# Making the split weight blocks of four tail pairs anew in the second half of a Strassen projection, instead of storing and reloading them

## The chip, the cores and the metric

One core of one Trainium2 chip runs the whole program. The metric is the time of one execution on the device in microseconds. The kernel before takes 2260.27 us, the median of 3 runs (2259.36 to 2262.28).

## What is computed

One layer of a residual decoder block on a sequence of 2048 rows of width 1024, in float32. Cut to what matters here:

```
h    = rms_norm(x) * (1 + scale) + shift
proj = h @ w_in                      # 1024 x 8192
x_rnn, z_rnn, q, k, v, z_attn, g_r, g_a = split(proj)
y_rnn  = (rg_lru(conv(x_rnn)) * silu(z_rnn)) @ w_out_rnn
y_attn = (dilated_attention(rope(q), rope(k), v) * silu(z_attn)) @ w_out_attn
merged = sigmoid(g_r) * y_rnn + sigmoid(g_a) * y_attn
out    = rms_norm(x + gate * (merged @ w_o))
```

The change touches only how the operands of `h @ w_in` and of `merged @ w_o` are prepared.

## The kernel before

**The products.** A float32 product is made of three passes over a high and a low part (`mm3`, L152). The high part is a rounded copy made on ACT (`hi_act`, L158), the low part a difference made on POOL (`lo_pool`, L164). All of `proj` but the values v is computed in 28 "pairs" of two 128-column blocks, by a Strassen scheme of 7 products a pair (`strassen`, L362; 12 matmuls of 128x512 each, L150, accumulated in PSUM tiles X, Z, W, V, Y). The sequence is done in two halves, f = 0 and f = 1, with the same 28 pairs, so that each half has 196 products, one after the other on PE. The first sums of a pair leave PSUM as tile u1 on ACT (L399) before the fifth product can use X again.

**The pairs.** Pairs 0 to 21 are the recurrent branch with the gates in between; the tail, pairs 22 to 27, makes q and k. In the tail (`TAIL_ROTATED`), pairs 23 and 25 hold the rotary columns, eight pieces of 32 columns (they go through `split` for all seven operands and are stored whole), and 22, 24, 26 and 27 are "plain", with blocks of one or two pieces of columns.

**The left operands.** In the first half they are made from the weight (`operand_events`, L265): four raw blocks of 256 KB loaded on SP (tiles R, L253), sums on DVE (s1, s2, L289, L290, and two in place, L298 and L303), seven splits (tiles S), each placed `LEAD` = 4 products ahead of its use. The splits are then stored to DRAM (sD, 512 KB each) from ACT's queue, each two splits after it was made (L281; the last two in a flush, L284). Operands 0, 4 and 5 of a pair that is not rotated are not stored (`PLAIN`), since they are split copies of raw blocks. In the second half `load_next` (L317) brings each operand into a ring of seven S tiles as soon as the product seven before it is done: from sD (L325), or the raw block (L253) with its split four products ahead (`split_next`).

**Between the halves** `second_values` (L863) computes v for the second half in eight runs (`value_runs`, L840). A run's two PSUM tiles are copied on ACT (ev, L767) and stored with four DMAs on SP (vN, L769) after the first quarter of the next run. The four first loads of the ring are in the plan at the first quarter of run 7, three more in the quarters behind.

**In the second half** two more jobs are spread between products: `output_weights` (L436) splits the output weights by way of the tiles s1 and s2 and stores them, 32 parts, one in 19/4 products; `gated_weight` (L1299) loads four groups of `w_o` (tiles wo, ws), multiplies them by the gate on DVE (L1315), forms Strassen sums, and stores them to oD (L1331, L1332) from ACT's queue. The groups begin 1, 10, 19 and 28 products into the tail.

**Queues.** SP and ACT issue their DMAs in program order. The compiled program gives each DMA of the two queues one of eight semaphores in turn (DMAHW0 to 7 in its waits), and a DMA first waits for the earlier DMA that holds the same one. A store on ACT's queue that waits so holds up all that ACT has behind it.

Of the kernel before, what the change touches and what calls it, by code (L numbers as in the profile page):

```python
# [10 lines left out]
F32 = mybir.dt.float32  # L11
# [4 lines left out]
ALU = mybir.AluOpType  # L16
# [4 lines left out]
P = 128  # L21
# [4 lines left out]
CH = 512  # L26
# [63 lines left out]
def decoder_block(ctx, tc, x, c, positions, g_norm, w_mod, b_mod, w_in, b_gate, conv_w, conv_b,  # L90
# [170 lines left out]
    LEAD = 4  # L261
    PLAIN = {0: (0, 0), 4: (0, 1), 5: (1, 1)}
    loaders, unsplit = {}, []

    def operand_events(x, pieces):  # L265

# [7 lines left out]

        def split(i, name):
            first[7 * x + i] = t = split_s(v[name])
            if i not in PLAIN or x not in loaders:
                kept.append((7 * x + i, t))
            if len(kept) > 2:
                k, t2 = kept.pop(0)  # L280
                nc.scalar.dma_start(sD[k], t2[:].bitcast(F32))  # L281
            while 7 * x + i == 28 * 7 - 1 and kept:
                k, t2 = kept.pop(0)
                nc.scalar.dma_start(sD[k], t2[:].bitcast(F32))  # L284
# [54 lines left out]


    def split_next(n):
        while unsplit and unsplit[0][0] <= n:
            _, t, r = unsplit.pop(0)
            hi_act(t[:, 0], r)
            lo_pool(t[:, 1], r, t[:, 0])
# [16 lines left out]
    def strassen(up, f, key, done):  # L362
# [8 lines left out]
        def take():  # L371
            if f:
                return (f, *loaded.pop(0))
            i = next(n_op)
            return f, i, first.pop(i)

        def prod(ps, b, first, last, op=None):
            f, i, s = op or take()
            bh, bl = B[b]
            for k in range(KH):  # L380
                mm3(ps[:], s[:, 0, k, :], s[:, 1, k, :], bh[:, k, :], bl[:, k, :],
                    first=first and k == 0, last=last and k == KH - 1, skip_group_check=True)
            n_prod[0] += 1
            if f:
                used.add(i)
                while n_loaded[0] - NS in used:
                    load_next()
                split_next(i + 4)
            run_late(n_prod[0])

        X = T(pj, [P, CH], F32, "X", bufs=2)
# [44 lines left out]
    def output_weights():  # L436

        parts = [(i, w, m, half) for i, w in enumerate((w_out_rnn, w_out_attn)) for m in range(KT) for half in range(2)]
        for x, (i, w, m, half) in enumerate(parts):
# [17 lines left out]
            for d, fn in ((1, load), (4, split), (6, store)):  # L457
                after_prod.setdefault(n_prod[0] + 19 * x // 4 + d, []).append(fn)

# [403 lines left out]
    def second_values():  # L863
# [5 lines left out]
        for i in range(4):  # L869
            for t in range(7):  # L870
                if t == 3:
                    plan[t, i].append(lambda i=i: load_piece(0, i))
                else:
                    n = t + 1 if t < 3 else t - 4
                    plan[t, i].append(lambda n=n, i=i: split_piece(n, i))
                    if n not in (2, 3) or t == 1:
                        plan[t, i].append(lambda n=n, i=i: load_piece(n + 1, i))
            plan[7, i].append(lambda i=i: [load_next() for _ in range(4 if i == 0 else 1)])
        plan[7, 2].append(lambda: split_next(0))
# [419 lines left out]
    def gated_weight(ep):  # L1299
# [5 lines left out]
        def group(k):  # L1305
# [11 lines left out]
            def sums(i):  # L1317
                if not i:
                    v["t"] = T(ep, [P, 3, CH], F32, "ws")
                    v["t3"] = T(wq, [P, KH, P], F32, "s1", bufs=1)  # L1320
# [72 lines left out]
    for f in range(2):  # L1393
# [15 lines left out]
        if f:  # L1409
            output_weights()  # L1410

        pump()
# [864 lines left out]
```

## Time and profile before

| | |
|---|---|
| median of 3 runs | 2260.27 us |
| profiled execution, its own time | 2258.11 us |
| its span | 2256.0 us |
| mean granted clock of TensorE | 0.992 |
| PE busy | 2201.3 us (98%) |
| DVE, ACT, POOL busy | 1456.7, 1294.0, 1215.1 us |
| DMA | 520.19 MB, mean 231 GB/s |
| stores of splits to sD, loads from it | 118 and 118, 512 KB each |

The first half's products end at 720 us or so, the values of the second half run until 829.6, and the second half's products from there until 1409. Attention, the output products and the last norm follow. A row of the timeline gives the start, the length, the engine with the line and the operation, the tiles written and read, and in brackets how long the engine stood idle before it and what ended that.

### The profile page before, as it was taken

The page shows a single profiled execution, that of the slowest core. Times are in us where ns is not written, and L with a number is a line of the kernel's source. Part 1 is how long each engine was busy: PE and PEld are TensorE (multiplying, and loading weights), DVE is VectorE, ACT ScalarE, POOL GpSimd, SP SyncE. Part 2 cuts the span into 40 slices and gives each one's busy share as a digit, 9 for nine tenths or more (in the row PEclk, how much of TensorE's full clock was granted, in tenths as well). Part 3 has the DMA queues.
Part 4 walks back from the last instruction along what each step waited for, and adds up shares of the span by engine and source line. Part 5 has one row for each costly group of instructions (what it writes and reads, how often), then busy time and mean ns, then how long its engine had stood idle before and what let it go on. Part 6 is the DMA issues. An engine that isn't in the chain of part 4 may idle for free.

```text
span 2256.0 us, 34354 instructions
## 1 busy us (share of the span) xinstructions
PE 2201.3 (98%) x11359; PEld 1845.6 (82%) x11359; DVE 1456.7 (65%) x2451; ACT 1294.0 (57%) x2560; POOL 1215.1 (54%) x902
## 2 busy tenths in 40 slices
PE   8999999999999999999999999999999999999898
PEld 5998888888877988888888887888989898977786
DVE  5578788778557664555645455467677878645776
ACT  3547767678533436666766611477677887632333
POOL 2277677676556344445445312356565656433786
PEclk9999999999999999999999999999999999999999
DMA  8354665565797647877787899989988888788553
GB/s 283 90 171 165 204 212 179 189 228 189 233 268 230 219 138 224 260 233 237 241 256 237 261 309 296 298 266 289 272 280 264 241 261 257 234 275 260 174 168 131
DMA packets 455433, 520.19 MB, mean 231 GB/s; under 512 B 90360, under 2 KB 333268, under 8 KB 454232
## 3 DMA queue, kind: packets, MB, share of 16 engines
q1 hardware_dynamic: 427492, 434.95, 63.6%
q10 hardware_dynamic: 27572, 83.00, 9.7%
q8 instruction: 90, 1.47, 0.3%
q14 instruction: 87, 0.71, 0.1%
q0 software_dynamic: 192, 0.05, 0.0%
HBM read 340.67 MB, written 177.21 MB: 230 GB/s over the span
## 4 chain that ended last, share of the span: by engine, by line
PE 48%; DMA 10%; DVE 3%; issue 3%; ACT 2%; POOL 2%; SPq 1%; ACTq 0%; POOLq 0%; DVEq 0%
PE X L150 9%; PE pj L150 9%; PE V L150 7%; PE W L150 4%; PE Z L150 4%; PE Y L150 4%; PE sc L150 4%; PE o L150 4%; DMA fg<-mrT 1%; DMA meT<-fg 1%; PE pg L150 1%; PE pT L1628 1%; DMA wo<-in_w_o_dram 1%; PE pT L1641 1%; DMA R<-in_w_in_dram 1%
## 5 line engine op out<-in xcount | busy, mean ns | idle before, releaser
L164 POOL TENSOR_TENSOR S<-R,S 128x512 fp32r<-128x512 f32 x278 | 408.2, 1473 | 402.8 <-ACT S L158 361.4
L150 PE MATMUL X<-T,S 128*128 128x512 f32 x1344 | 334.8, 398 | 10.4 <-ACT S L158 5.2
L150 PE MATMUL V<-T,S 128*128 128x512 f32 x1344 | 331.2, 395 | 0.0
L150 PEld LDWEIGHTS X<-T,S 128*128 128x128 f32 x1344 | 255.0, 190 | 72.1 <-ACT S L158 5.9
L150 PEld LDWEIGHTS V<-T,S 128*128 128x128 f32 x1344 | 252.3, 188 | 58.3 <-DVE ev L466 0.3
L150 PE MATMUL pj<-yh,S 128*128 128x512 f32 x848 | 287.8, 397 | 4.6 <-DMA S<-wD 3.9
L158 ACT ACTIVATE S<-R 128x512 fp32r<-128x512 f32 x278 | 170.7, 622 | 134.5 <-DMA R<-in_w_in_dram 111.8
L164 POOL TENSOR_TENSOR S<-s,S 128x512 fp32r<-128x512 f32 x108 | 165.9, 1537 | 128.7 <-ACT S L158 97.0
L150 PEld LDWEIGHTS pj<-yh,S 128*128 128x128 f32 x848 | 160.9, 190 | 37.9 <-DVE fg L1859 4.3
L1544 ACT ACTIVATE pp<-pp,st 128x256 f32<-128x256 f32 (+3 forms) x256 | 133.4, 523 | 75.2 <-DVE st L1543 74.8
L150 PE MATMUL pj<-yl,S 128*128 128x512 f32 x424 | 167.5, 395 | 2.1 <-DVE yl L167 1.2
L150 PE MATMUL Y<-T,S 128*128 128x512 f32 x672 | 165.5, 395 | 0.0
L150 PE MATMUL Z<-T,S 128*128 128x512 f32 x672 | 165.4, 395 | 0.0
L150 PE MATMUL W<-T,S 128*128 128x512 f32 x672 | 165.3, 395 | 0.0
L150 PEld LDWEIGHTS Z<-T,S 128*128 128x128 f32 x672 | 126.6, 188 | 29.7
L150 PEld LDWEIGHTS Y<-T,S 128*128 128x128 f32 x672 | 126.6, 188 | 29.3
L150 PEld LDWEIGHTS W<-T,S 128*128 128x128 f32 x672 | 126.4, 188 | 29.3
L158 ACT ACTIVATE S<-s 128x512 fp32r<-128x512 f32 x108 | 67.3, 623 | 109.7 <-DVE s L290 35.1
L167 DVE TENSOR_TENSOR ptl<-pT,pth 128x384 fp32r<-128x384 f32 (+1 forms) x160 | 97.8, 628 | 49.3 <-ACT pth L158 47.1
L960 DVE SCALAR_TENSOR_TENSOR xc<-xr,par,xc 128x512 f32<-128x512 f32 x96 | 96.6, 1006 | 50.2 <-ACT xc L954 48.0
L1543 DVE CUSTOM_DVE_ANT_0 pp<-sc,msk 128x256 f32<-128x256 f32 (+3 forms) x256 | 104.2, 449 | 37.2 <-PE sc L150 35.0
L164 POOL TENSOR_TENSOR kq<-kraw,kq 128x512 fp32r<-128x512 f32 (+1 forms) x64 | 101.3, 1593 | 41.7 <-ACT kq L158 41.7
(382 smaller groups left out, 4841.6 us busy)
## 6 DMA issues: line engine op xcount, KB each, us to landing
sD<-S ACTq DMA_DIRECT2D x118, 512.0 KB, 3.7
S<-sD SPq DMA_DIRECT2D x118, 512.0 KB, 5.1
S<-wD SPq DMA_DIRECT2D x100, 512.0 KB, 5.7
R<-in_w_in_dram SPq DMA_DIRECT2D x196, 256.0 KB, 4.1
wD<-s ACTq DMA_DIRECT2D x64, 256.0 KB, 4.9
T<-in_w_mod_dram SPq DMA_DIRECT2D x8, 1024.0 KB, 12.0
vN<-ev SPq DMA_DIRECT2D x64, 128.0 KB, 2.8
zaT<-ev SPq DMA_DIRECT2D x32, 256.0 KB, 2.8
```

The costliest lines, as they stand in the source:

```text
L150: nc.tensor.matmul(o, lhsT=l, rhs=r, start=st, stop=sp, **kw)
L158: nc.scalar.activation(o, i, AF.Copy)
L164: nc.gpsimd.tensor_tensor(o, i, h.bitcast(F32), ALU.subtract)
L167: nc.vector.tensor_tensor(o, i, h.bitcast(F32), ALU.subtract)
L960: nc.vector.scalar_tensor_tensor(xc, xr[:, i : i + CH], cw(i), xc, ALU.mult, ALU.add)
L1543: nc.vector.tensor_tensor_reduce(pdst, s_ps, mask, 1.0, 3e38, ALU.add, ALU.min, m_)
L1544: nc.scalar.activation(pdst, pdst, AF.Exp, bias=m_, scale=-1.0, accum_out=l_)
L1628: nc.tensor.transpose(pt[:, c0 + j * P : c0 + (j + 1) * P], pp[i][:, k * P : (k + 1) * P], ident)
L1641: nc.tensor.transpose(pt[:, c * P : (c + 1) * P], pp[:, half * P : (half + 1) * P], ident)
```

## The change

The operands of the plain tail pairs (`ANEW` = 22, 24, 26, 27) are not stored in the first half, and the second half makes them once more by `operand_events`, with raw loads, sums and splits 4 products ahead; the ring of loads pauses inside these pairs (`load_free`). `output_weights` goes at one part in 9/2 products instead of 19/4, so that the tiles s1 and s2 are free before pair 22. `second_values` puts three of the ring's first loads at the end of run 6's plan. `gated_weight` writes two of its sums in place in the wo tile, stores 2 times 512 KB a group, and its groups begin at 1, 11, 21 and 31.

```
+    ANEW = (22, 24, 26, 27)
...
         def split(i, name):
+            if f:
+                assert n_loaded[0] == 7 * x + i
+                n_loaded[0] += 1
             first[7 * x + i] = t = split_s(v[name])
-            if i not in PLAIN or x not in loaders:
+            if x not in ANEW and (i not in PLAIN or x not in loaders):
                 kept.append((7 * x + i, t))
-            if len(kept) > 2:
-                k, t2 = kept.pop(0)
-                nc.scalar.dma_start(sD[k], t2[:].bitcast(F32))
-            while 7 * x + i == 28 * 7 - 1 and kept:
+            while len(kept) > 2 or kept and x >= ANEW[0] and kept[0][0] < 7 * x + i - 1:
...
+    def load_free():
+        n = n_loaded
+        while n[0] - NS in used and not (n[0] < 28 * 7 and n[0] // 7 in ANEW):
+            load_next()
...
-                while n_loaded[0] - NS in used:
-                    load_next()
+                load_free()
                 split_next(i + 4)
             run_late(n_prod[0])
+            if f:
+                load_free()
+                split_next(i + 4)
...
-                after_prod.setdefault(n_prod[0] + 19 * x // 4 + d, []).append(fn)
+                after_prod.setdefault(n_prod[0] + 9 * x // 2 + d, []).append(fn)
...
-            plan[7, i].append(lambda i=i: [load_next() for _ in range(4 if i == 0 else 1)])
+            plan[7, i].append(load_next)
+        plan[6, 3].append(lambda: [load_next() for _ in range(NS - 4)])
...
-                    tt(v["t3"][:].rearrange("p k m -> p (k m)"), b22, b12, ALU.subtract)
-                    tt(t[:, 2, :], b21, t[:, 1, :], ALU.subtract)
+                    tt(b22, b22, b12, ALU.subtract)
+                    tt(b21, b21, t[:, 1, :], ALU.subtract)
...
-                nc.scalar.dma_start(oD[k, :, :3, :], v["t"][:])
-                nc.scalar.dma_start(oD[k, :, 3, :], v["t3"][:].rearrange("p k m -> p (k m)"))
+                nc.scalar.dma_start(oD[k, :, :2, :], v["t"][:])
+                nc.scalar.dma_start(oD[k, :, 2:, :], v[1][:])
...
-        for k, i in enumerate((1, 10, 19, 28)):
+        for k, i in enumerate((1, 11, 21, 31)):
...
         if f:
             output_weights()
+            for x, (_, pieces) in enumerate(pair_order()):
+                if x in ANEW:
+                    events.extend((28 * 7 + 7 * x + d - LEAD, 15 * x + i, fn)
+                                  for i, (d, fn) in enumerate(operand_events(x, pieces, f)))
+            events.sort(key=lambda e: e[:2])
```

Three places show how the instructions move. The first is SP's queue between the values and the second half's first product; vN are the stores of a run's values, R the raw block of the ring's operand 0, S1 to S3 its operands from sD. Before, with the stores of runs 5 and 6 ahead of every load:

```order
L769 DMA vN<-ev_1324_7800 128x2x128
L769 DMA vN<-ev_1324_7800 128x2x128
L769 DMA vN<-ev_1334_7939 128x2x128
L769 DMA vN<-ev_1334_7939 128x2x128
L769 DMA vN<-ev_1335_7943 128x2x128
L769 DMA vN<-ev_1335_7943 128x2x128
L253 DMA R3_1337_7948<-in_w_in_dram 128x4x128
L325 DMA S1_1338_7950<-sD 128x1024
L325 DMA S2_1339_7952<-sD 128x1024
L325 DMA S3_1340_7954<-sD 128x1024
```

The same place of the changed kernel:

```order
L777 DMA vN<-ev_1324_7784 128x2x128
L777 DMA vN<-ev_1324_7784 128x2x128
L253 DMA R3_1332_7889<-in_w_in_dram 128x4x128
L326 DMA S1_1333_7891<-sD 128x1024
L326 DMA S2_1334_7893<-sD 128x1024
L777 DMA vN<-ev_1338_7930 128x2x128
L777 DMA vN<-ev_1338_7930 128x2x128
L777 DMA vN<-ev_1339_7934 128x2x128
L777 DMA vN<-ev_1339_7934 128x2x128
L326 DMA S3_1340_7938<-sD 128x1024
```

The first three loads now stand ahead of run 6's four stores; the fourth and later ones stay behind them.

The second is ACT's queue at the end of the first half: the last splits of pair 27, the stores sD, and u1 of pair 27, which PE waits for. Before:

```order
L158 ACTIVATE S_1155_6624<-R_1122_6401 128x512
L158 ACTIVATE S_1163_6657<-s_1137_6498 128x512
L281 DMA sD<-S_1144_6550 128x1024
L284 DMA sD<-S_1147_6576 128x1024
L284 DMA sD<-S_1163_6657 128x1024
L399 ACTIVATE u_1164_6663<-X_6582 128x512
L535 ACTIVATE T_6617<-pg_6642,mod_233,gs_234 128x512
```

The changed kernel:

```order
L158 ACTIVATE S_1155_6611<-R_1122_6392 128x512
L158 ACTIVATE S_1163_6644<-s_1137_6488 128x512
L407 ACTIVATE u_1164_6647<-X_6569 128x512
L543 ACTIVATE T_6604<-pg_6629,mod_233,gs_234 128x512
```

The three stores ahead of u1 are gone. In the same way the four stores each of pairs 22, 24 and 26 are gone from ACT's queue; the seven each of pairs 23 and 25 stay.

The third is ACT's queue in the second half, around the third group of `gated_weight`; t and u are copies out of PSUM. Before:

```order
L399 ACTIVATE u_2253_12525<-X_12466 128x512
L158 ACTIVATE S_2248_12500<-R_2249_12501 128x512
L1118 ACTIVATE t_2266_12590<-X_12466 128x512
L1331 DMA oD<-ws_12544 128x1536
L1332 DMA oD<-s_2258_12545 128x512
L158 ACTIVATE S_2263_12583<-R_2264_12584 128x512
L158 ACTIVATE S_2268_12605<-R_2269_12606 128x512
L399 ACTIVATE u_2282_12687<-X_12614 128x512
```

The changed kernel, from the u1 of the same pair on:

```order
L407 ACTIVATE u_2258_12537<-X_12479 128x512
L158 ACTIVATE S_2263_12559<-R_2241_12420 128x512
L158 ACTIVATE S_2266_12579<-s_2262_12556 128x512
L158 ACTIVATE S_2271_12605<-R_2245_12451 128x512
L1127 ACTIVATE t_2273_12611<-X_12479 128x512
L158 ACTIVATE S_2275_12629<-s_2261_12555 128x512
L158 ACTIVATE S_2280_12658<-R_2257_12534 128x512
L1339 DMA oD<-ws_12599 128x1024
L1340 DMA oD<-wo_12494 128x1024
L158 ACTIVATE S_2281_12677<-R_2249_12474 128x512
L158 ACTIVATE S_2285_12703<-s_2262_12556 128x512
L407 ACTIVATE u_2287_12709<-X_12637 128x512
```

A plain tail pair has seven splits on ACT where it had three, and the two stores to oD now stand ahead of two of them and of the next u1.

More of the change, by code (lines that the diff above doesn't have):

```diff
@@ L262, in decoder_block, with operand_events @@
     PLAIN = {0: (0, 0), 4: (0, 1), 5: (1, 1)}
+    ANEW = (22, 24, 26, 27)
     loaders, unsplit = {}, []
-    def operand_events(x, pieces):
+    def operand_events(x, pieces, f=0):
         load, v = block_loads(pieces), {}
@@ L371, in take @@
         def take():
-            if f:
+            if f and x not in ANEW:
                 return (f, *loaded.pop(0))
@@ L1318, in sums @@
                 if not i:
-                    v["t"] = T(ep, [P, 3, CH], F32, "ws")
-                    v["t3"] = T(wq, [P, KH, P], F32, "s1", bufs=1)
+                    v["t"] = T(ep, [P, 2, CH], F32, "ws")
                 t = v["t"]
```

## The prediction

> **What bounds the kernel now.** I read the page's busy times first.
>
> ```profile
> span 2256.0 us, 34354 instructions
> PE 2201.3 (98%) x11359; PEld 1845.6 (82%) x11359; DVE 1456.7 (65%) x2451; ACT 1294.0 (57%) x2560; POOL 1215.1 (54%) x902
> ```
>
> PE is busy for 2201.3 of 2256.0 us. The change takes no matmul away, so it can win only from some 55 us of idle time and from matmuls that ran at a reduced clock. Next come windows of 40 us around the tails (columns: PE, PEld, DVE, ACT, POOL busy; granted clock; DMA share; GB/s).
>
> ```profile
> 600.00:640.00 40.00, 35.65 (x149) 28.50 (x148) 10.09 (x15) 12.54 (x22) 17.46 (x13) 0.97 0.95 281
> 640.00:680.00 40.00, 40.00 (x172) 32.40 (x171) 28.99 (x36) 17.33 (x31) 27.53 (x18) 0.99 0.88 259
> 800.00:840.00 40.00, 34.98 (x263) 33.21 (x262) 27.13 (x25) 14.38 (x26) 19.35 (x12) 0.91 0.43 132
> 1320.00:1360.00 40.00, 40.00 (x174) 32.45 (x173) 27.90 (x38) 5.85 (x10) 10.32 (x7) 1.00 0.84 273
> 1360.00:1400.00 40.00, 38.98 (x167) 31.02 (x166) 22.01 (x32) 5.84 (x10) 13.63 (x10) 1.00 0.96 289
> ```
>
> In the second half's tail (1320 to 1360) PE is full: the transfers saved there shorten nothing by themselves. PE is short at 600 to 640, 800 to 840 and a little after 1360. The timeline of PE names each gap in brackets.
>
> ```profile
> 637.18 4.61 PE L150 MATMUL X<-T,S 128*128 128x512 f32 x12 [4.35 <-ACT u L399]
> 721.41 0.66 PE L525 MATMUL pg<-cs,x 128*128 128x128 f32 x4 [3.00 <-DVE t L545]
> 834.47 5.38 PE L150 MATMUL X<-T,S 128*128 128x512 f32 x12 [4.89 <-ACT S L158]
> 839.68 2.48 PE L150 MATMUL Z<-T,S 128*128 128x512 f32 x10
> 1366.04 0.74 PE L150 MATMUL X<-T,S 128*128 128x512 f32 x2 [0.35 <-ACT S L158]
> 1367.45 2.59 PE L150 MATMUL X<-T,S 128*128 128x512 f32 x10 [0.67 <-POOL S L164]
> 1406.12 2.96 PE L150 MATMUL V<-T,S 128*128 128x512 f32 x12
> 1408.92 0.39 PE L150 MATMUL pj<-yh,S 128*128 128x512 f32 x1
> 1410.46 0.50 PE L150 MATMUL pj<-yl,S 128*128 128x512 f32 x1 [1.16 <-DVE yl L167]
> 1412.53 0.80 PE L150 MATMUL pj<-yh,S 128*128 128x512 f32 x1 [0.63 <-ACT yh L158]
> ```
>
> A product without a gap takes 2.96 us and is followed 2.80 us after its start (1406.12 to 1408.92). Below, each gap is priced against that.
>
> **A, the first product of the second half.** PE ended the values at 834.47 − 4.89 = 829.58, and product Z began at 839.68: 10.10 us for one product, so 7.3 lost. SP, ACT and SP's waits show why.
>
> ```profile
> 811.60 18.20 SPq L769 DMA_DIRECT2D vN<-ev x8
> 829.89 0.44 SPq L253 DMA_DIRECT2D R<-in_w_in_dram  x1
> 831.92 1.50 SPq L253 DMA_DIRECT2D R<-in_w_in_dram  x2
> ```
> ```profile
> SPq L769 <- ACT ev L767: 15.5, 2, 14.2
> ```
> ```profile
> 827.72 0.59 ACT L767 ACTIVATE ev<-X 128x512 f32<-128x512 f32 x1
> 833.79 0.63 ACT L158 ACTIVATE S<-R 128x512 fp32r<-128x512 f32 x1 [5.48 <-DMA R<-in_w_in_dram]
> 839.45 0.63 ACT L158 ACTIVATE S<-R 128x512 fp32r<-128x512 f32 x1 [4.07 <-DMA R<-in_w_in_dram]
> ```
>
> SP stood in the stores of runs 5 and 6 from 811.60 to 829.8; 14.2 us of it is one wait, of run 6's first store for its copy out of PSUM (the last row, of the waits: in all, times, longest), and the last copy ended at 828.31. Without the wait, eight stores take 4 us. The first raw block was issued at 829.89, landed about 833.8, and its split came 4.2 us too late for PE. In the changed order this load and two of sD stand ahead of run 6's stores; behind run 5's four, 2 us, they are issued near 814 and land before 822 even at twice their 4 us. The split then stands directly behind the copy that ends at 828.31: high part done at 828.94, ahead of PE's 829.58, low part a POOL operation (1.47 us, row below) later at 830.4. The first matmuls use only the high part, so PE waits 0.2 to 0.8 us. **Gain 6.8**, bounds 5 and 7.3.
>
> What is late next: the blocks that stay behind run 6's stores. Four stores from 828.3 on, the fourth sD load, and two raw blocks come out at about 830 to 831.5. Before, the raw blocks took from 831.92 to 839.45 to be there. With the same 7.5 us they would be split at 839.6, and the fifth product needs them at 829.6 + 0.3 + 4 × 2.8 = 841. That covers it by 1.4 us, and the three loads in front of them are gone by then.
>
> **B, pair 23 in the first half.** The gap of 4.35 us and a product of 4.61 instead of 2.96 make 6.0 us. ACT's rows:
>
> ```profile
> 636.16 0.33 ACTq L281 DMA_DIRECT2D sD<-S  x1
> 636.53 0.60 ACT L399 ACTIVATE u<-X 128x512 f32<-128x512 f32 x1 [4.73 <-DMA R<-in_w_in_dram]
> 715.14 4.05 ACTq L284 DMA_DIRECT2D sD<-S  x2
> 719.24 0.60 ACT L399 ACTIVATE u<-X 128x512 f32<-128x512 f32 x1 [5.17 <-DMA kT<-t]
> 720.57 0.63 ACT L158 ACTIVATE S<-R 128x512 fp32r<-128x512 f32 x1
> ```
>
> A store to sD waited for the raw load that held its semaphore, and u1, which PE waited for, stood behind the store. This is a store of pair 23, which the change keeps, and in the compiled order it still waits for the same load. What goes are the four stores of pair 22 just ahead. The DMA view from 600 to 740 prices them.
>
> ```profile
> q10 hardware_dynamic: 4493, 16.32, 30.8%
> sD<-S ACTq DMA_DIRECT2D x30, 512.0 KB, 4.4
> R<-in_w_in_dram SPq DMA_DIRECT2D x11, 256.0 KB, 6.2
> ```
>
> ACT's queue takes 30.8% of 140 us for 16.32 MB: 2.64 us of all engines per MB. Four stores (2.1 MB) are 5.5 us less work in a stretch whose DMA share is 0.95, and this works back through ACT's and SP's earlier waits. The store must be free 4.35 us sooner to close the gap. I take **4.0**, between 0 (the load's own issue and latency set it) and 6.0.
>
> **C, the end of the first half.** PE waited 3.00 us for the first turned tile of the values, and DVE for ACT's row at 719.24, whose 5.17 us lay behind the two flush stores and the one ahead of them. All three vanish with pair 27's stores, and u1 then runs when X is done. Next on ACT is the value weight's split at 720.57, behind a load; it moves up with the load and isn't the first thing PE needs. **Gain 2.7**, bounds 1.5 and 3.0.
>
> **E, the second half's tail.** Pair 26 waited 0.35 + 0.67 us for a late raw block; made anew, it is loaded earlier: **1.0**, bounds 0 and 1.0. At the change to the output products, windows of 2 us show a low clock.
>
> ```profile
> 718.00:720.00 2.00, 0.41 (x2) 0.00 (x0) 0.13 (x1) 0.76 (x2) 0.00 (x0) 1.00 0.99 286
> 832.00:834.00 2.00, 0.00 (x0) 0.00 (x0) 0.00 (x0) 0.21 (x1) 0.00 (x0) 0.54 0.99 295
> 1412.00:1414.00 2.00, 1.48 (x3) 0.94 (x4) 1.49 (x3) 1.98 (x4) 0.00 (x0) 0.60 1.12 347
> 1414.00:1416.00 2.00, 2.00 (x7) 1.57 (x6) 2.00 (x4) 1.21 (x3) 0.00 (x0) 0.54 0.98 220
> ```
>
> The two last cost 2 × 0.40 + 2 × 0.46 = 1.7 us at clocks 0.60 and 0.54, and ACT's wait for a load at 1412.53 another 0.63; the pauses of DVE just before stay. The tail moves less data, so these loads should land sooner. **Gain 1.5**, bounds 0 and 2.3. In the clock's rows, the 3.00 us pause before 721.41 kept it at 1.00, the 4.89 us one brought 0.54. The Trainium skill ("TensorE: Matmul & The Clock Gate", What's actually happening) says that the clock is halved after an idle window of about 3.4 us. The pauses of 3.00 and 4.89 agree with it; 1412 to 1416 does not, with single pauses no longer than 1.2 us between short matmuls. By the rule the low clock there would not come from these pauses, nor go with them: E would keep 0.6 of its 1.5, and the sum would be 0.9 smaller. The measurement decides, and I keep 1.5.
>
> **What is added.** A plain pair of the second half (seven products, 19.6 us) gains four splits and four sums.
>
> ```profile
> L164 POOL TENSOR_TENSOR S<-R,S 128x512 fp32r<-128x512 f32 x278 | 408.2, 1473 | 402.8 <-ACT S L158 361.4
> L158 ACT ACTIVATE S<-s 128x512 fp32r<-128x512 f32 x108 | 67.3, 623 | 109.7 <-DVE s L290 35.1
> L290 DVE TENSOR_TENSOR s<-s,R x28: 691/693/1772, 143.3 to 700.6; 128x512 f32<-128x512 f32 x28
> S<-sD SPq DMA_DIRECT2D x118, 512.0 KB, 5.1
> ```
>
> That is 4 × 0.62 = 2.5 us on ACT, 4 × 1.47 = 5.9 on POOL and 4 × 0.69 to 1.77 = 2.8 to 7.1 on DVE. At two such pairs in 40 us, POOL's 10.32 becomes about 22, ACT's 5.85 about 11, DVE's 27.90 at most 42 if every sum ran at its longest, and 34 at the shortest. The first half's tail did the same splits and the same rotation with POOL at 27.53, ACT at 17.33 and DVE at 28.99 while PE stayed at 40.00 (640 to 680). Splits are made four products, 11 us, ahead. The data falls from 4 × 512 + 3 × 256 = 2816 KB a pair to 1024 KB.
>
> New waits: SP, issuing a pair's last raw block, waits until its buffer is free, up to 5 us; behind it stand loads of the next rotated pair and of w_o, five products ahead. ACT's stores to oD now have splits and u1 behind them. In-place sums and the later group starts ride on DVE and ACT between products; the stores of output weights come 7.5 products sooner in the whole half, under full PE. Between nothing (the work is hidden) and 3 us (one gap like C) I take **1.5 lost**.
>
> **Sum.** −6.8 − 4.0 − 2.7 − 1.0 − 1.5 + 1.5 = −14.5 us. Against the profiled execution, 2258.11, that gives 2243.6; this execution is 2.2 below the median of the runs, 2260.27, on which I put the forecast: **2245.8 us**. All gains at their upper bounds (7.3 + 6.0 + 3.0 + 1.0 + 2.3 = 19.6) give 2240.7; all at their lower (5 + 1.5 = 6.5) and 3 lost give 2256.8.
>
> **Rivals.** A difference of 0.2%, 4.5 us, is about what a measurement can tell from no change: faster is below 2255.8, slower above 2264.8.
>
> 1. *Only A is realised.* Pairs 23 and 25 keep their stores, so B's store is as late as before and u1 at C finds another limit (the value weight's load at 720.57). For: the blocking pair 23 stays, and its store waits for the same load. Against: 0.95 DMA share loses 5.5 us of work just ahead. −6.8 + 1.5 = −5.3, 2255. Chance 0.12, half of it within 0.2%.
> 2. *The second half's tail is blocked as the first was: slower.* A store to oD waits for a load's semaphore while splits and u1 stand behind it, 6.0 us each as at B, at four groups: 24 lost, against A, B and C's 13.5: 2270.8. From three blocked groups (18 us) on it decides. For: B and C are this mechanism, and the stores now stand ahead of splits. Against: the same eight stores were there before with PE at 40.00, and data there falls by more than half. Chance 0.10.
> 3. *The early loads don't serve A.* If SP still waits (a slot of S or R freed late by the values' matmuls or POOL), the split stays late and 6.8 is missing: −7.7, 2252.6. Against: the matmuls that free the slots ended by about 815. Chance 0.08, a quarter of it within 0.2%.
>
> The forecast has 0.70, all of it faster. Faster: 0.70 + 0.06 + 0.06 = 0.82; same 0.06 + 0.02 = 0.08; slower 0.10. The range 2239 to 2257 takes in the bounds and rivals 1 and 3, a little over 0.8.
>
> **What would show it.** A: PE's first product of the second half within 1 us of the values' end, and no clock of 0.5 there; SP's first raw load ahead of run 6's stores, near 814. B: ACT's u1 of pair 23 less than 1 us late. C: no stores ahead of pair 27's u1. Second half: POOL at 20 to 25 of 40 us with PE at 40.00, and less than 1.0 DMA share between 1280 and 1400. The prediction is wrong if a PE gap of over 3 us with a release by ACT's split or u1 stands between 1300 and 1400, or if B's gap keeps its length.

## The result

| | before | changed |
|---|---|---|
| median of 13 runs each | 2261.59 us | 2253.07 us |
| lowest to highest | 2258.55 to 2264.80 | 2250.93 to 2258.08 |
| span of the profiled execution | 2256.0 us | 2249.2 us |

The ratio is 0.9966, with a 95% interval of 0.9957 to 0.9974: 6 to 10 us faster, where 14.5 were forecast. The time lies inside the forecast's range, but the gain is little over half of the forecast.

The same windows of 40 us as in the prediction, of the changed kernel (columns as there):

```profile
600.00:640.00 40.00, 40.00 (x174) 32.43 (x173) 15.21 (x21) 14.06 (x26) 18.94 (x15) 1.00 0.95 270
640.00:680.00 40.00, 40.00 (x174) 32.44 (x173) 32.05 (x43) 16.52 (x30) 27.62 (x19) 1.00 0.73 193
800.00:840.00 40.00, 39.70 (x251) 35.56 (x250) 21.20 (x23) 16.63 (x30) 18.40 (x13) 1.00 0.69 208
1320.00:1360.00 40.00, 37.39 (x153) 29.43 (x152) 24.70 (x35) 6.31 (x12) 11.01 (x8) 0.96 0.83 245
1360.00:1400.00 40.00, 35.69 (x146) 28.29 (x145) 33.56 (x36) 7.77 (x14) 24.76 (x15) 0.96 0.62 181
```

The two holes of before, at 600 to 640 and at 800 to 840, are filled. Two new ones stand where PE was full, or nearly: 2.6 us at 1320 to 1360, 4.3 at 1360 to 1400. PE's timeline names the gaps; no other of over 0.3 us is left from pair 23 to the last product.

```profile
820.23 2.58 PE L150 MATMUL X<-T,S 128*128 128x512 f32 x10 [0.30 <-POOL S L164]
1332.39 4.44 PE L150 MATMUL X<-T,S 128*128 128x512 f32 x12 [2.42 <-DMA S<-sD]
1366.55 3.02 PE L150 MATMUL V<-T,S 128*128 128x512 f32 x12 [1.72 <-DVE t L474]
1388.90 4.49 PE L150 MATMUL V<-T,S 128*128 128x512 f32 x12 [2.60 <-ACT S L158]
1406.01 0.50 PE L150 MATMUL pj<-yh,S 128*128 128x512 f32 x1 [1.34 <-ACT yh L158]
```

The first row is all that is left of A. The next three are the first product of pair 25, and the fourth of pairs 26 and 27. Against a product of 2.96 us they cost 2.42 + 1.48, 1.72 + 0.06 and 2.60 + 1.53: 9.8 us together.

**A ledger of the stages.** PE's 11359 weight loads come in the same order in every kernel here, so the start of the k-th, minus its start in before, tells how far a kernel is ahead there. I read it at loads 1000 (151 us in before), 3500 (734, behind the first half's products), 4500 (886, behind the first product of the second half), 6750 (1408, the last product), 7000 (1462, behind the change from these products to the output products, called the change of stage) and at the last load; the table has the difference made in each stretch, in us, with one profiled execution of each kernel. The first column, up to 1.3, is the start.

```
                                          first   first    second   change
                                   to     half's  product  half's   of
kernel                             151    tail    (A)      tail     stage   rest    end
changed kernel                    -1.3    -8.8    -6.9      9.8      0.7    -0.6   -7.1
e1  early loads only              -0.7    -1.0    -6.9     -0.2      2.3     1.3   -5.1
e2  groups at 1, 10, 19, 28        0.3    -9.3    -6.7      4.4      4.2    -0.1   -7.3
e3  loads first                    0.0    -9.3    -6.7      4.3      2.8    -0.6   -9.5
e4  both                          -0.5    -9.5    -6.7      4.0      4.4     2.4   -6.1
e5  e3, no gate work, groups 3, 4 -0.7    -9.5    -6.7     -0.8     -1.5     3.1  -16.0
e6  anew 22, 27                   -1.1    -9.5    -6.8      0.3      3.5     1.7  -11.9
e7  anew 22                       -0.9    -8.3    -6.7      0.0      2.1     0.6  -13.3
e8  anew 22, 24, 26               -0.1    -7.5    -6.8      2.9      3.3     3.0   -5.1
e9  e7, groups at 1, 10, 19, 28   -0.6    -3.9    -6.7      2.3      1.0     2.1   -5.9
e10 e6, groups at 1, 10, 19, 28   -0.1    -9.5    -6.7      4.8      2.9     2.0   -6.6
e11 e7, loads not first           -0.8    -4.4    -6.9      0.9      4.1     3.9   -3.2
e12 nothing anew                  -0.2    -5.9    -7.0     -0.9      1.0     6.2   -6.8
e13 before, sooner stores         -0.5    -7.2    -0.2      0.5      2.4     1.4   -3.6
e14 before, early loads + sooner  -0.5    -4.2    -6.8      0.5      0.8     1.8   -8.4
e15 e7, gate on POOL               0.3    -8.3    -6.8      3.9      1.5     0.5   -8.9
```

How far one row can be trusted shows in rows with the same instructions in the first half: e1 and before differ by 1.0 in its tail; e7, e9, e11 and e15 have 8.3, 3.9, 4.4 and 8.3; the seven kernels with 22 and 27, or all four, made anew 8.8 to 9.5. The last column is one execution. For the whole time the ratios below decide, which come from 4 to 21 runs a side. Before was run again beside each set of kernels, and kernels are compared by their ratios to it. A ratio is not the quotient of the two medians beside it: for e11 that would be 0.9950 instead of 0.9961.

### The profile page after: what moved, and what is told of

Same layout as the page of the kernel before. It is cut to its first block, busy times and chain, and to the rows that moved or that the text cites. A ratio compares the mean times of both kernels' runs of the same rounds, so it can differ in the third digit from the quotient of the medians.

```text
span 2249.2 us, 34373 instructions
## 1 busy us (share of the span) xinstructions
PE 2200.1 (98%) x11358; PEld 1845.6 (82%) x11359; DVE 1492.8 (66%) x2467; ACT 1302.8 (58%) x2576; POOL 1247.9 (55%) x918
## 5 line engine op out<-in xcount | busy, mean ns | idle before, releaser
L164 POOL TENSOR_TENSOR S<-R,S 128x512 fp32r<-128x512 f32 x282 | 419.2, 1491 | 343.7 <-ACT S L158 294.6
L164 POOL TENSOR_TENSOR S<-s,S 128x512 fp32r<-128x512 f32 x120 | 185.9, 1549 | 148.4 <-ACT S L158 101.9
L158 ACT ACTIVATE S<-s 128x512 fp32r<-128x512 f32 x120 | 74.8, 624 | 157.7 <-DVE s L291 84.1
L1621 ACT ACTIVATE pp<-pp,M 128x256 f32<-128x256 f32 (+3 forms) x256 | 118.1, 524 | 9.2 <-DVE M L1745 9.2
```

Source lines behind the costliest of these rows:

```text
L158: nc.scalar.activation(o, i, AF.Copy)
L164: nc.gpsimd.tensor_tensor(o, i, h.bitcast(F32), ALU.subtract)
L1621: nc.scalar.activation(pp, pp, AF.Copy, scale=w)
```

## The experiments

My theory after the result: A, B and C came as forecast; the second half's tail lost them again by two mechanisms of its own. *Order on SP:* pair 25's operands come late because their loads stand behind stores that wait for DVE. *DVE full:* the groups of the gated weight and the remade sums together fill DVE, and PE waits for DVE to read V. The rival was the prediction's own second one: ACT held by the stores to oD.

SP's queue in the changed kernel, and the longest waits of SP from 1296 to 1335 (in all, times, longest):

```profile
1304.53 1.04 SPq L1321 DMA_DIRECT2D wo<-in_w_o_dram  x2
1317.20 8.44 SPq L1161 DMA_DIRECT2D qT<-t  x8
1325.76 2.73 SPq L326 DMA_DIRECT2D S<-sD  x4
```
```profile
SPq L1161 <- DVE t L1158: 14.9, 2, 11.6
```

The loads of pair 25 pause while pair 24 is made anew, and then stand behind eight stores of the rotated q, two of which wait 14.9 us for DVE. The first is issued at 1325.76, lands at 1332.35, and PE starts at 1332.39. DVE ahead of the third gap:

```profile
1382.45 1.72 DVE L1324 TENSOR_TENSOR wo<-wo,gb 128x1024 f32<-128x1024 f32 x1
1384.09 1.78 DVE L1332 TENSOR_TENSOR ws<-wo 128x512 f32<-128x512 f32 x1
1385.90 1.65 DVE L1333 TENSOR_TENSOR ws<-wo,ws 128x512 f32<-128x512 f32 x1
1387.47 0.68 DVE L304 TENSOR_TENSOR s<-R,s 128x512 f32<-128x512 f32 x1
1388.08 0.68 DVE L474 TENSOR_TENSOR t<-V,u 128x512 f32<-128x512 f32 x1
```
```profile
1368.00:1392.00 24.00, 21.40 (x89) 16.99 (x88) 23.77 (x24) 4.43 (x8) 18.06 (x11) 0.96 0.58 156
```

DVE is busy for 23.77 of 24 us. Its read of V (L474) ends at 1388.76, and PE's next V starts at 1388.90. The timeline puts that gap down to ACT's split of S, which ended 0.02 us before PE's start; but that split is of operand 6, used three products later. By the compiled order this matmul waits for the read of V. Ahead of the second gap it is the same: DVE works without a pause from 1354.36 on, its read of V ends at 1366.40, and PE starts at 1366.55.

```profile
1364.03 1.77 DVE L304 TENSOR_TENSOR s<-R,s 128x512 f32<-128x512 f32 x1
1365.72 0.68 DVE L474 TENSOR_TENSOR t<-V,u 128x512 f32<-128x512 f32 x1
```

The stores to oD of groups 3 and 4 on ACT's queue:

```profile
1356.39 0.33 ACTq L1339 DMA_DIRECT2D oD<-ws  x1
1359.33 0.33 ACTq L1340 DMA_DIRECT2D oD<-wo  x1
1388.30 0.33 ACTq L1339 DMA_DIRECT2D oD<-ws  x1
1391.08 0.33 ACTq L1340 DMA_DIRECT2D oD<-wo  x1
```

Group 3's were gone seven microseconds before the second gap ended, and group 4's first was issued when DVE's read of V was already under way. So neither gap is one of ACT held by a store.

**e1, the early loads alone.**

```
-            plan[7, i].append(lambda i=i: [load_next() for _ in range(4 if i == 0 else 1)])
+            plan[7, i].append(load_next)
+        plan[6, 3].append(lambda: [load_next() for _ in range(NS - 4)])
```

> The kernel before with the one edit that puts the second half's first loads ahead of the last values' stores. My theory: of the changed kernel's gains this is A alone, about -7 us against before (the gap of 4.89 us before the second half's first product and its half clock go), while the gaps of 4.35 us at pair 23, 3.00 us at pair 27 and 0.35 + 0.67 us at pair 26 stay as they are. Rival (the early loads push the gap to a later load): less than 4 us, with a new gap among the first five products of the half.

Measured 2251.33 against 2259.12, ratio 0.9969 (0.9956 to 0.9982). PE's gaps in the tails:

```profile
635.11 3.05 PE L150 MATMUL X<-T,S 128*128 128x512 f32 x12 [2.81 <-ACT u L399]
718.23 0.66 PE L525 MATMUL pg<-cs,x 128*128 128x128 f32 x4 [2.72 <-DVE t L545]
1358.79 2.59 PE L150 MATMUL X<-T,S 128*128 128x512 f32 x10 [0.67 <-POOL S L164]
```

A came as expected and is gained whole; the other gaps stayed, if not at their lengths. This one edit has as much net gain as the whole change (0.9969 against 0.9966). B's gap is 2.81 us here with no slow clock behind it, where the same instructions in before had 4.35 and 1.65 more: its price of 6.0 was that of one execution. C's gap of 2.72 us, on the other hand, was followed by a granted clock of 0.50 (720 to 722), where it stayed at 1.00 in before, so that this tail as a whole is only 1.0 us ahead.

**e2, e3 and e4, the two mechanisms.** e2 moves the groups, e3 puts a product's loads ahead of the rotation's stores, e4 does both.

```
-        for k, i in enumerate((1, 11, 21, 31)):
+        for k, i in enumerate((1, 10, 19, 28)):
```
```
                 load_free()
                 split_next(i + 4)
+                if i >= 21 * 7:
+                    pump()
+                    load_free()
             run_late(n_prod[0])
```

> The changed kernel with the groups of the gated weight back at 1, 10, 19 and 28 instead of 1, 11, 21 and 31. Theory (DVE is the bound late in the second half's tail, since the gated weight's multiplications and sums of groups 3 and 4 stand beside the remade sums of pairs 26 and 27): the gaps of 1.72 us (pair 26) and 2.60 us with its half clock (pair 27) shrink or go, 3 to 6 us faster than the changed kernel; the gap of 2.42 us at pair 25 stays. Rival (ACT held by the stores of the gated weight): the gaps go along with the stores, no more than 1 us gained.

> The changed kernel, where in the second half's tail the operand events and the ring's loads of a product are put ahead of the work that is due then (the rotation and its stores), so that the loads of pair 25's first two operands stand ahead of four of the eight stores of the rotated q on SP. Theory (pair 25's first operand comes late since its load stands behind these stores, which wait for DVE): the 2.42 us gap at pair 25 and its half clock go, about 3.9 us faster than the changed kernel, and the two later gaps stay. Rival (the transfers themselves are slow, or the slot comes free late): the gap keeps more than half of its length.

> The changed kernel with both edits (groups at 1, 10, 19, 28; loads ahead of the due work). Theory: the three gaps are separate and the gains add, 7 to 10 us faster than the changed kernel, 15 to 18 us faster than before. Rival (one engine, DVE, is full, and a gap that is closed comes back in the next pair): not more than the better of the two single edits plus 1 us.

Measured against 2259.12: e2 2251.47, ratio 0.9964 (0.9951 to 0.9977); e3 2248.76, 0.9956 (0.9942 to 0.9971); e4 2251.44, 0.9963 (0.9949 to 0.9977). PE's gaps in e2, then in e3:

```profile
1324.06 3.03 PE L150 MATMUL V<-T,S 128*128 128x512 f32 x12 [1.66 <-DVE t L474]
1375.97 3.06 PE L150 MATMUL V<-T,S 128*128 128x512 f32 x12 [1.29 <-DVE t L474]
1386.35 3.02 PE L150 MATMUL V<-T,S 128*128 128x512 f32 x12 [1.74 <-ACT S L158]
1405.49 0.80 PE L150 MATMUL pj<-yh,S 128*128 128x512 f32 x1 [3.18 <-ACT yh L158]
```
```profile
1364.60 4.59 PE L150 MATMUL V<-T,S 128*128 128x512 f32 x12 [2.50 <-DVE t L477]
1403.01 0.79 PE L150 MATMUL pj<-yh,S 128*128 128x512 f32 x1 [2.86 <-ACT yh L158]
```

e3 did what the order on SP predicts: the gap at pair 25 is gone. By the ratios it is some 2 us better than the changed kernel, where 3.9 were expected, and the intervals overlap. Of the two later gaps, which were to stay, pair 27's went and pair 26's grew from 1.72 to 2.50 us with a slow product behind it. e2 missed: gaps of 1.66, 1.29 and 1.74 us stand at pair 24, at pair 26's last product and at pair 27. Pair 25's gap went too, but not because its load came sooner: that was issued at 1328.68 behind the same eight stores and landed at 1332.53, just as PE, held up at pair 24, came to it at 1332.57. Its tail is 5.4 us better in the ledger, and 3.5 us of that are lost at the change of stage, where a wait for yh has grown to 3.18. e4 fits the rival that was written for it: closing both gaps was worth no more than one.

**e5, DVE's work left out.** In e3, groups 3 and 4 lose their multiplications and sums.

```
             def store_sums():
-                nc.scalar.dma_start(oD[k, :, :2, :], v["t"][:])
+                nc.scalar.dma_start(oD[k, :, :2, :], v["t"][:] if k < 2 else v[0][:])
...
+            if k > 1:
+                return (0, load), (8, store_sums)
```

> The kernel with the loads first (e3), with the six DVE operations of each of the gated weight's groups 3 and 4 left out: the loaded weight is stored as it is. This leaves out the gating and the Strassen sums of half of the output weight, and keeps all loads and stores. Theory (the gap left in that kernel, 2.50 us at pair 26, is PE waiting for DVE's read of V behind this work): the gap goes, and the second half's products end 3 to 4 us sooner. But part of it is given back behind the products, since the first loads of the output products set that stage's start: 0 to 2 us faster than e3 in all. Rival (ACT held by the stores to oD, which stay): the gap stays.

Measured 2239.46 against 2259.03, ratio 0.9912 (0.9896 to 0.9927). The windows of e5:

```profile
1320.00:1360.00 40.00, 39.72 (x171) 31.67 (x170) 26.95 (x41) 8.01 (x14) 16.43 (x12) 1.00 0.93 277
1360.00:1400.00 40.00, 38.84 (x169) 31.25 (x168) 21.61 (x28) 9.71 (x18) 13.11 (x9) 1.00 0.84 261
```

All stores to oD are there, and no gap of over 0.3 us is left in the tail: this decides for DVE's work. (The stores no longer wait for sums either; that ACT held by them wasn't the cause is read from the times in the changed kernel above.) The second half of the expectation missed, to the good: not 0 to 2 but some 9 us faster than e3. The change of stage gains 1.5 us instead of losing 2.8. So that loss went with DVE's work too. My reading is that the first loads of the output products stand on SP behind stores of the rotated k, and that those wait for DVE: SP's waits for DVE from 1365 to 1400 add up to 6.8 us in e3 and to 4.7 in e5.

**e6, e7 and e8, which pairs are made anew:** 22 and 27 in e6, 22 in e7, 22, 24 and 26 in e8, all with the loads first (the last stores are flushed at the half's end where pair 27 is stored). The edit of e6:

```
-    ANEW = (22, 24, 26, 27)
+    ANEW = (22, 27)
```

> The kernel with the loads first, with only pairs 22 and 27 made anew; 24 and 26 are stored and loaded as before. Theory: the first half keeps both gains (the gap at pair 23 needs only pair 22's stores gone, the one at pair 27 only its own), the second half has half of the remade sums, so the DVE gap at pair 26 goes and a gap like before's at pair 26 (0.35 + 0.67 us) comes back: 12 to 14 us faster than before. Rival (the first half needs all sixteen stores gone): the gap of 3 to 4 us at pair 23 or at pair 27 returns.

> The kernel with the loads first, with only pair 22 made anew. Theory: A and B stay (-6.9 and -6.2 us), C's gap of about 3 us at pair 27 is back, no DVE gap in the second half's tail, and the loads of the output products start as early as before: 10 to 13 us faster than before. Rival (B's gap is closed by less traffic of all four pairs): the gap at pair 23 returns, no more than 8 us faster.

> The kernel with the loads first, with pairs 22, 24 and 26 made anew and 27 stored. Theory: A and B stay, C is back, the 2.50 us gap at pair 26 stays since pair 26's sums still stand beside group 3, and the loads of the output products are no longer behind pair 27's splits: 8 to 11 us faster than before. It tells whether making pair 27 anew, worth 3 us in the first half, gives that back at the change to the output products: if so, this is no slower than e3; if not, it is 3 us slower.

Measured against 2259.03: e6 2247.18, ratio 0.9943 (0.9930 to 0.9955); e7 2245.39, 0.9938 (0.9926 to 0.9951); e8 2252.98, 0.9970 (0.9958 to 0.9982). PE's gaps in e7:

```profile
712.13 0.66 PE L536 MATMUL pg<-cs,x 128*128 128x128 f32 x4 [0.90 <-DVE t L556]
1351.41 2.59 PE L150 MATMUL X<-T,S 128*128 128x512 f32 x10 [0.67 <-POOL S L164]
1398.20 0.79 PE L150 MATMUL pj<-yh,S 128*128 128x512 f32 x1 [2.37 <-ACT yh L158]
```

e6 came out as expected in time and e7 a little better: with two pairs or one, the first half keeps its gain, and the second half's tail loses nothing. Not every gap is where it was expected: C's is 0.90 us in e7 instead of about 3, and e6 has 1.44 us by DVE at pair 27 instead of 0.35 + 0.67 at pair 26. e7 is the only complete kernel besides e6 whose interval lies below the changed kernel's. e8 was a little below what was expected; it keeps the DVE gap (2.58 us) and has C's back in part (1.56). It is slower than e3 by 3 us in the ratios, the sign that pair 27 made anew is worth its cost, but the intervals overlap, and e6 against e7 shows no such worth.

**e9, e10 and e11, variations of e6 and e7.** e9 is e7 and e10 is e6 with the groups at 1, 10, 19, 28; e11 is e7 without the loads first.

> The kernel with only pair 22 made anew (e7), with the groups of the gated weight at 1, 10, 19 and 28. Theory: the wait of 2.37 us at the change to the output products comes from SP, whose loads for them stand behind stores of the rotated k that wait for DVE; with group 4 three products sooner DVE is free sooner there: 1 to 3 us faster than e7. Rival (those loads are bound by the DMAs' rate, not by SP): no difference, within 1 us.

> The kernel with pairs 22 and 27 made anew (e6), with the groups at 1, 10, 19 and 28. Theory: the DVE gap of 1.44 us at pair 27 goes and the wait of 4.02 us at the change to the output products shrinks: 2 to 4 us faster than e6, and 0 to 2 us faster than e7, since C is gained in full. Rival (pair 27's own splits hold the output products' loads up): the gap goes, but the 4 us wait stays or grows, within 1 us of e6.

> The kernel with only pair 22 made anew (e7), without putting the loads first. Theory: the late load in the changed kernel came in pair 24's pause of the ring, which isn't there now, and pair 22's pause was covered: within 1 us of e7. Rival (every pause of the ring costs): a gap of about 2.4 us at pair 23, 3 to 4 us slower than e7.

Measured against 2258.22: e9 2247.77, ratio 0.9964 (0.9952 to 0.9977); e10 2251.72, 0.9969 (0.9960 to 0.9978); e11 2246.98, 0.9961 (0.9947 to 0.9975). e9 and e10 missed: the sooner group is no gain. In e9 the wait of 2.37 us is down to 1.25, but pair 26's gap, 0.67 in e7, has grown to 1.07 + 0.69. The reason given for that wait isn't borne out by e7's own trace: from 1365 to 1400 SP waits there 1.4 us in all for DVE, and 7.4 us for other DMAs. In e10 a gap of 1.98 us at pair 27 and a wait of 3.60 at the change of stage stand where e6 had 1.44 and 4.02. In e11 pair 23 has no gap, as the theory said, but its time is nearer to e9's than to e7's. In the ledger 4 to 5 us of the distance from e9 and e11 to e7 arise in the first half, where the three are the same instruction by instruction. The profiled executions of e9 and e11 were also the slowest of their five. So e7's lead over them isn't shown to come from an edit.

**e12, nothing made anew**, the rest of e3 kept (`ANEW` holds no pair).

> The kernel with the loads first and no pair made anew: all splits are stored and loaded as before, the rest of the change stays (early loads, spacing of the output weights, gated sums in place, groups at 1, 11, 21, 31, and stores in the tail one split sooner). Theory: A stays, the gap at pair 23 is back with 3 to 4.4 us, the one at pair 27 with 1 to 3: 6 to 8 us faster than before, 5 to 7 us slower than e7. Rival (the stores one split sooner are what closes the gap at pair 23): within 1 us of e7.

Measured 2249.62 against 2258.22, ratio 0.9965 (0.9953 to 0.9978). As much as expected, but the reason failed: the gap at pair 23 is closed though all its neighbours' stores are there. The rest of the change has one thing that touches them. In the tail, `split` now issues a store when its split is two splits old, of any kind; before, two later *stored* ones had to be made. In a plain pair that is sooner.

**e13 and e14, the sooner stores alone, and with the early loads.**

```
-            if len(kept) > 2:
-                k, t2 = kept.pop(0)
-                nc.scalar.dma_start(sD[k], t2[:].bitcast(F32))
-            while 7 * x + i == 28 * 7 - 1 and kept:
+            while len(kept) > 2 or kept and (x >= 22 and kept[0][0] < 7 * x + i - 1 or 7 * x + i == 28 * 7 - 1):
```

> The kernel before with one edit: in the tail a split's store is issued as soon as two later splits of any kind are made, instead of when two later stored splits are (in a plain pair with its three unstored splits that is one or two products sooner). Nothing is made anew and all 118 stores stay. Theory A (the gap at pair 23 comes from pair 22's stores standing close ahead of pair 23's on ACT, and spreading them is enough): the gap of 4.35 us goes, the gap at pair 27 shrinks from 3.0 to 1 to 2 us, 4 to 7 us faster than before. Theory B (the traffic of pair 22's stores must be gone, as the prediction had it, and the closed gap without remade pairs had another reason): the gap at pair 23 stays over 3 us, less than 2 us faster.

> The kernel before with two edits only: the second half's first loads ahead of the last values' stores, and the tail's stores issued sooner. Nothing is made anew. Theory A (the change's gain is A plus the place of the stores, and remaking the sixteen operands has cost in the second half what it won in the first): 10 to 13 us faster than before, so faster than the changed kernel. Theory B (remaking is what closes the gap at pair 23): 7 us faster, as with the early loads alone.

Measured against 2257.48: e13 2257.28, ratio 0.9997 (0.9986 to 1.0007); e14 2252.39, 0.9973 (0.9963 to 0.9984). In e13's profile pair 23 has no gap at all, pair 27's is

```profile
713.69 0.66 PE L522 MATMUL pg<-cs,x 128*128 128x128 f32 x4 [1.35 <-DVE t L542]
```

and the first half's tail is 7.2 us ahead; e14 has 0.86 and 1.68 us there, 1.43 more at pair 24, and is 4.2 ahead. Yet e13's runs show no gain, and e14's are those of e1. Theory A holds for the gap and theory B for the time. The profiled e13 gave 2.4 us back at the change of stage and ended 3.6 us ahead. That is well within the spread of single executions (before alone: 2252.65 to 2263.49), so what the closed gap is worth in an average run isn't shown.

**e15, the gate on POOL.** In e7, the multiplications of groups 3 and 4 run on POOL.

```
-                tt(v[i][:].rearrange("p j c -> p (j c)"), v[i][:].rearrange("p j c -> p (j c)"), gate_b[:], ALU.mult)
+                (tt if k < 2 else nc.gpsimd.tensor_tensor)(
+                    v[i][:].rearrange("p j c -> p (j c)"), v[i][:].rearrange("p j c -> p (j c)"), gate_b[:], ALU.mult)
```

> The kernel with only pair 22 made anew (e7), with the four multiplications by the gate of the gated weight's groups 3 and 4 on POOL instead of DVE (nothing is left out). Theory: at the change to the output products PE waits for loads that stand on SP behind stores of the rotated k, and these wait for DVE; POOL is free at 7 of 40 us there, so DVE comes 5 us of work sooner and the wait of 2.4 us shrinks: 1 to 3 us faster than e7. Rival (a POOL operation slows the DVE sums beside it, as in the changed kernel, where sums took 1.77 instead of 0.68 us under POOL): no gain, or up to 3 us slower.

Measured 2251.14 against 2257.49, ratio 0.9966 (0.9953 to 0.9979): slower than e7 by twice what the rival allowed, and level with e9 and e11. The wait at the change of stage did shrink, from 2.37 to 1.85 us, but a new gap stands ahead of it. PE, then POOL's multiplications, then DVE:

```profile
1385.24 4.60 PE L150 MATMUL V<-T,S 128*128 128x512 f32 x12 [3.58 <-DVE t L477]
```
```profile
L1327 POOL TENSOR_TENSOR wo<-wo,gb 128x1024 f32<-128x1024 f32 x4 | 9.6, 2394 | 12.3 <-DMA wo<-in_w_o_dram 12.3
```

```profile
1376.56 0.69 DVE L1336 TENSOR_TENSOR ws<-wo 128x512 f32<-128x512 f32 x1 [3.44 <-POOL wo L1327]
1382.85 1.73 DVE L1337 TENSOR_TENSOR ws<-wo,ws 128x512 f32<-128x512 f32 x1 [5.59 <-POOL wo L1327]
1384.51 0.68 DVE L477 TENSOR_TENSOR t<-V,u 128x512 f32<-128x512 f32 x1
```

A multiplication takes POOL 2.39 us. DVE stands idle for 5.59 us until the second one is done, makes one sum, and only then reads V, until 1385.19; PE starts at 1385.24, 3.58 us late. DVE is busy for 19.98 of the 40 us from 1360 to 1400 there, so it is not full. So the rival had the outcome but not the reason: what held DVE was above all the wait for POOL's result in its own queue, with the read of V behind it; the sum slowed by POOL (1.73 us) added about one microsecond.

## Why the prediction was wrong

**A was right in mechanism and size:** forecast 6.8, in the ledger 6.9, in e1's runs 7.0 (0.31% of 2259.12). The first raw block went out behind run 5's stores (805.43), its split was ready in time, PE waited 0.30 us for the low part, and no clock of 0.5 followed.

**B and C, together 6.7 forecast, were 8.8 in the profile, for a reason only partly as stated.** The prediction put B down to 5.5 us less work of the DMAs, pair 22's stores being gone. e12 and e13 close the same gap, and e14 all but 0.86 us of it, with these stores still made, only sooner. So the traffic need not go; the place of the stores on ACT is enough. With 22 and 27 not stored the gain is steady (8.8 to 9.5 in seven executions), with the sooner stores it is 4.2 to 7.2 in three, so some of it belongs to their absence. C's gap is gone in all seven, and 0.72 to 2.10 us in the eight that store pair 27 sooner, so it is pair 27's absence that is steady. How large B is in an average run of before stays open: one other execution of the same instructions (e1) had 2.81 us for 6.0, and e13 closed the gap without a gain in its runs. That B and C came out above their forecast and made up for some of the loss below is in part luck.

**E failed.** 1.0 came (pair 26's gap of before is gone); the other 1.5, sooner loads at the change of stage, did not. PE waits there 1.16 and 1.34 us, and the ledger loses 0.7.

**The step that failed is "I take 1.5 lost"** under what is added; the second half's tail measured 9.8. The sign given for it, PE at 40.00, failed in both windows (37.39 and 35.69). Two sentences led to it.

- *DVE.* The prediction added two pairs' sums to the window 1320 to 1360 and compared that with the first half's tail, where PE stayed at 40.00. But the first half has no gated weight, whose groups 3 and 4 meet pair 26's and 27's sums in the window behind. There DVE went to 33.56 of 40 and to 23.77 of 24 us. e5 shows that this work is what decides: without it no gap is left, and the time falls by some 9 us. It is the two together, and not the later start of the groups: with the groups back in place the tail still loses 4.4 us (e2) or 4.0 (e4; 4.3 in e3 with late groups), and with late groups but nothing remade (e12) it loses none.
- *SP.* The wait of the ring's loads was named ("behind it stand loads of the next rotated pair") and set aside as five products ahead. The queue in front of them was not read to its end: eight stores of pair 23's rotated q, which wait for DVE. e3 moves the loads ahead of four of them: the first lands at 1326.65 instead of 1332.35, and the 3.9 us at pair 25 are gone.

The second rival (ACT held by the stores to oD, 6.0 a group) had the place right and the engine wrong: no store stands ahead of the two gaps by DVE, and e5 keeps the stores and has no gap.

**What the change is worth, part by part.** The early loads alone give 0.9969; the change without any pair made anew 0.9965; the whole change 0.9966. Remaking sixteen operands gains about 9 us in the first half and loses as much in the second, where its sums stand beside the gated weight's on DVE. With pair 22 alone remade, and the loads first, the ratio is 0.9938 (0.9926 to 0.9951), better than both kernels; but three kernels close to it (e9, e11, e15) lie at 0.9961 to 0.9966, so a safe reading is 0 to 6 us better than the changed kernel. Open is also why a lead of 7 to 17 us at the last product shrinks by 1 to 4 us at the change of stage in all but e5: that the output products' first loads wait behind DVE on SP is argued from SP's order and from e5, was not tried by moving those loads, and does not fit e7, where SP hardly waits for DVE.

## What to carry to other kernels

Work that moves from one stage to another must be added to what the other stage does *at its busiest window*, with every engine's queue read to the end: here DVE was a third free on average and full for 24 us. A load's slack counts from its place in its queue, not from the product ahead of which it was planned; a store that waits for a slow engine takes that slack from all loads behind it. And where one execution's gaps differ by 4 us with the same instructions, the part of a change that is to be credited has to be run alone: here one edit of three lines alone gains as much as the whole change.

## What the runs showed of the hardware

**DVE beside POOL.** A sum of two 128x512 tiles takes 0.68 us alone and up to 1.8 while POOL works. The groups of one sum in the changed kernel, from 1260 to 1400 (min/median/max ns):

```profile
L1332 DVE TENSOR_TENSOR ws<-wo x4: 676/680/1777, 1288.3 to 1384.1; 128x512 f32<-128x512 f32 x4
L1154 DVE TENSOR_TENSOR t<-t,St x8: 692/1612/1803, 1311.9 to 1376.8; 128x512 f32<-128x512 f32 x8
```

In that stretch the sums of two SBUF tiles that POOL's work covers for over nine tenths took 1.78 us in the median (13 of them, 0.69 to 1.80), those that it doesn't touch 0.69 (19, at most 0.69). DVE's reads of PSUM, with only one tile from SBUF, took 0.67 to 0.69 us under POOL too (11). So splits added to POOL mostly lengthen DVE's sums beside them, which the prediction had as an upper bound and didn't take. The Trainium skill ("GPSIMD Engine Reference", 1. Specifications) states that POOL shares its interfaces to SBUF with VectorE and contends with DVE instructions that have two SBUF inputs; these numbers agree.

**The clock after a pause.** A pause of a given length sometimes halves the clock of the next product and sometimes does not. The same place in e4, then in e10:

```profile
1384.86 3.04 PE L150 MATMUL V<-T,S 128*128 128x512 f32 x12 [1.98 <-ACT S L158]
```
```profile
1384.67 4.57 PE L150 MATMUL V<-T,S 128*128 128x512 f32 x12 [1.98 <-ACT S L158]
```

After 1.98 us the product took 3.04 us in the one and 4.57 in the other; 2.42, 2.50 and 2.60 us were followed by slow products here, 2.58 (e8) and 2.81 (e1) by full speed. So a gap of 2 to 3 us costs itself, and in some executions 1.5 us more. The Trainium skill ("TensorE: Matmul & The Clock Gate", What's actually happening) has a window of about 3.4 us that runs freely, and a half clock after an idle one. That the same pause can go both ways fits a window running freely; that 1.98 us is enough does not fit a window idle throughout.
